# Attention scores from one wide moving operand, their halves summed on VectorE, and one layer's probabilities normalised on ScalarE

## The chip, the cores and the metric

The kernel runs on one core of one Trainium2 chip. The metric is the device time of the whole program in microseconds (us); lower is better. A number that names a line, such as L211, is a line of the kernel file.

## What is computed

A decoder trunk of two layers over 256 tokens of width 2048, in float32. Layer 0 is "forgetting attention" with 32 heads of 64; layer 1 is sliding-window attention with 32 query heads that share 4 key/value heads. Cut to what matters:

```python
for i in range(2):
    h = rmsnorm(x, norm_g[i])
    p = h @ w_in[i]                       # q, k, v and a gate (and, in layer 0, a forget column per head)
    # layer 0: s = q k^T / 8 + c[t] - c[s], causal; softmax; times v
    # layer 1: s = rope(q) rope(k)^T / 8, window of 128, a learned sink in the softmax; times v
    y = attention(q, k, v) * silu(gate)
    x = x + y @ w_out[i]
return rmsnorm(x, final_g)
```

## The kernel before

**Matrix products.** Every float32 operand is split into a high part, rounded to the matmul's own format (fp32r), and a low part, the remainder. A product is three terms: high by high, high by low, low by high. A weight piece arrives by DMA; ScalarE rounds it (`load`, L210, a CAST), VectorE subtracts to get the low part (L211), and the two lie side by side in a tile `w`. In `block` (L216) one stationary operand multiplies high and low of the other side at once, 512 columns wide, and then the stationary low part multiplies the high part, 256 columns wide: for a weight part of four 128-row slices this is 4 matmuls of 512 columns and 4 of 256. Both go into one bank of PSUM, whose second half, the high-by-low term, is copied out by ScalarE (`low_half`, L257) and added by VectorE.

**The order of the work.** The weights are one stream of units of 256 output columns. A unit has four parts and two halves of output columns (c = 0 and 1, 128 each). The main loop at the end of the kernel calls `block(u, p, 0)` for a new part and then `block` of the part before it for half 1. After every second matmul `tick` advances a clock of steps and runs what has been put down for that step with `after`. So a block is four steps. A head pair's attention work is put down this way in `Pair.later`: scores at step s, the transposes of the first head's probabilities at step t, those of the second at t + 4, and for the whole group of two pairs the product with the values at a third step. The steps count from the moment that half 0 of the k unit (layer 0) or of the q unit (layer 1) is complete, and stand in the tables at the top: `FOX_DUE = ((16, 34), (40, 60), 106)` means pair 0 at s = 16, t = 34, pair 1 at s = 40, t = 60, values at 106. `FOX_FIRST` and `FOX_LAST` serve layer 0's first and last group, `SWA_LAST` layer 1's last. A group of layer 0 has four units (q, k, gate, v), 128 steps; a group of layer 1 has two (q, gate), 64 steps. TensorE's matmuls keep the order of the program; on VectorE and ScalarE a scheduler sets the order when the program is built, and both then run strictly in that order.

**From q to scores in layer 1.** When a half of the q unit is done, `rotate` (L691 to L697) adds the two halves of PSUM, shuffles, multiplies by the two rope tables and adds, and `stack_q` stacks the high and low parts of the 64 rows of each head over each other in 128 partitions: two copies on ScalarE (L329), two subtractions on VectorE (L330). Half c of the q unit holds the two heads of pair c. In layer 0 the keys are treated alike after `k` (L456 to L464).

**Scores to probabilities.** `score` multiplies, for each of the two query blocks and each of the two heads, q's stacked operand by the keys' high part and then, into the same place, by their low part. The first query block sees 128 keys and the second 256: four matmuls of 128 columns and four of 256 for a pair of heads. `biased` (L299) then reads the sum from PSUM, adds bias or mask, scales, writes the tile `st` to SBUF and keeps the row maximum: four instructions of VectorE. The exponentials are four ScalarE instructions (L309), the normalisation a reciprocal and four multiplications by a column on VectorE (L317, L320). TensorE transposes `st` (L76, into `pt`), ScalarE copies the result out (L363), and `values` multiplies it by v (into `psy`).

**Buffers.** The scores have two banks of PSUM (`ps_s`), the transposes two, the accumulators four.

Of the kernel before, what the change touches and what calls it, by code (L numbers as in the profile page):

```python
# [46 lines left out]
LOWEST = -3.4e38  # L47
SCALE = HD ** -0.5
# [3 lines left out]
def trunk(  # L52
# [16 lines left out]
    nc = tc.nc  # L69


    def mm(*args, **kw):
        tc.keep_in_program_order(nc.tensor.matmul(*args, **kw))  # L73
# [31 lines left out]
    def after(steps, fn):  # L105
        due.setdefault(clock[0] + max(steps, 1), []).append(fn)
# [82 lines left out]
    state = {}  # L189
# [26 lines left out]
    def block(unit, p, c):  # L216
# [14 lines left out]

        first, last = kt0 == 0, kt0 + s == KT
        ops = [operands(i) for i in range(s)]
        if unit.halves:

# [54 lines left out]

    BLK = ((slice(0, P), 0), (slice(P, 3 * P), 1))

    def biased(pss, bias, scale):

        st = work.tile([P, 2, 3 * P], F32, tag="st", name="st")
        mx = work.tile([P, 2, 2], F32, tag="mx", name="mx")
        for hh in range(2):
            for rng, qb in BLK:
                nc.vector.tensor_tensor_reduce(  # L299
                    out=st[:, hh, rng], in0=pss[hh][:, rng], in1=bias(hh, rng), scale=scale,  # L300
                    scalar=LOWEST, op0=ALU.add, op1=ALU.max, accum_out=mx[:, qb, hh : hh + 1],
                )
        return st, mx
# [11 lines left out]
    def normalise(st, l):  # L315
        rl = work.tile([P, 2, 2], F32, tag="rl", name="rl")
        nc.vector.reciprocal(rl, l)  # L317
        for hh in range(2):
            for rng, qb in BLK:
                nc.vector.tensor_scalar_mul(st[:, hh, rng], st[:, hh, rng], rl[:, qb, hh : hh + 1])  # L320

# [8 lines left out]
            nc.vector.tensor_sub(q2[other, hh, :], t[w, :], q2[w, hh, :].bitcast(F32))  # L330
        return q2

    def score(pss, q2, kk):

        for rng, qb in BLK:
            keys = rng.stop - rng.start
            for hh in range(2):
                q = q2[:, hh, qb * P : (qb + 1) * P]
                for part in range(2):
                    mm(  # L340
                        pss[hh][:, rng], q, kk[hh][:, part, 0:keys],
                        start=part == 0, stop=part == 1,
                    )

    class Pair:


        def __init__(self, j, scores, prepare=None):
            self.j, self.scores, self.prepare = j, scores, prepare

        def early(self):
            self.bias = self.prepare()

        def s(self):
            self.st = self.scores()

        def t(self, hh, group):
            pt = ps_t.tile([P, 512], F32, tag="T", name="pt")
# [4 lines left out]
            nc.scalar.copy(group.pts[hh][:, self.j, :], pt[:, 0 : 3 * P])  # L363

        def later(self, group, s, t):
            if self.prepare is not None:
                after(s - BIAS, self.early)
# [38 lines left out]
    ones_row, z, a = (once[0:H, i * S : (i + 1) * S] for i in range(3))  # L406
# [33 lines left out]
    class FoxGroup(Group):  # L440
# [13 lines left out]
        def k(self, c, ps):  # L454
# [32 lines left out]
        def pair(self, j):  # L487
            h0 = 4 * self.g + 2 * j

            def bias():  # L490

                assert "forgot" in state
                bc = fox.tile([P, 2, 3 * P], F32, tag="bc", name="bc")
                nc.gpsimd.dma_start(out=bc, in_=negc_d[h0 : h0 + 2, :].partition_broadcast(P))  # L494
                for hh in range(2):
                    diagonal = bc[:, hh, :].rearrange("p (b k) -> p b k", k=P)[:, 0:3:2, :]
                    fill_where_not(diagonal, [[0, 2], [-1, P]], 0, 1)
                return bc

            def scores():  # L500
                pss = [ps_s.tile([P, 512], F32, tag="S", name="ps_s") for _ in range(2)]
                kk = self.kT[j]
                score(pss, self.qT[j], (kk[:, 0], kk[:, 1]))
                bc = made.bias
                st, mx = biased(pss, lambda hh, rng: bc[:, hh, rng], 1.0)
# [4 lines left out]
                normalise(st, exps(st, mx))  # L510
                return st

            made = Pair(j, scores, bias)
            return made

        def v_of(self, j, b, hh):
            return self.vg[b][:, (2 * j + hh) * HD : (2 * j + hh + 1) * HD]
# [198 lines left out]
    class SwaGroup(Group):  # L716
# [6 lines left out]
        def q(self, c, ps):  # L723
# [3 lines left out]
            if c == 0:  # L727
                self.attend(2 * self.u, SWA_LAST if self.u == 7 else SWA_DUE, self.u == 7, True)

        def pair(self, j):  # L730
            h0 = 4 * self.u + 2 * j
            kv = self.u // 2

            def scores():
                pss = [ps_s.tile([P, 512], F32, tag="S", name="ps_s2") for _ in range(2)]
                kk = state["kk"][:, kv]
                score(pss, self.qT[j], (kk, kk))
                st, mx = biased(pss, lambda hh, rng: smask[:, rng], SCALE)
# [8 lines left out]
                normalise(st, l)  # L747
                return st

            return Pair(j, scores)  # L750

        def v_of(self, j, b, hh):
            kv = self.u // 2
# [53 lines left out]
    start = [(u, p) for p in range(3) for u in (v0, q0, k0)]  # L807
# [25 lines left out]
    smask = cpool.tile([P, 3 * P], F32, name="smask")  # L833
# [86 lines left out]
```

## Time and profile before

| | |
|---|---|
| median of 3 runs | 844.64 us (844.48 to 844.76) |
| the profiled execution, its own time | 844.48 us |
| its span, from first to last instruction | 842.7 us |
| TensorE (PE) busy | 830.0 us, 98% |
| VectorE (DVE) busy | 656.7 us, 78% |
| ScalarE (ACT) busy | 542.6 us, 64% |
| GpSimd (POOL) busy | 67.8 us, 8% |
| mean granted TensorE clock | 0.997 |
| moved by DMA | 150.51 MB, 179 GB/s on average |

In the rows of the timeline the first number is the start in us from the start of the span and the second the time that the row covers; "x8" means that eight like instructions of one engine were merged, and the row then bears the first one's form. The records of matmuls overlap (their ends are modelled), so the pace of TensorE is read from one start to the next. In the rows of groups the numbers behind the bar are busy us, mean ns of one instruction, and idle us of the engine before them with what ended it.

### The profile page before, as it was taken

How to read it: one execution, taken by the hardware profiler on the slowest of the kernel's cores; microseconds unless marked ns; L12 is line 12 of the kernel's file. 1: busy time of each engine (PE TensorE's matmuls, PEld its weight loads, DVE VectorE, ACT ScalarE, POOL GpSimd, SP SyncE). 2: the span in 40 equal slices, each digit the busy share in tenths (PEclk: the TensorE clock that was granted, in tenths of full speed). 3: DMA queues.
4: the chain of work that ended last, by engine and by line, in shares of the span. 5: the costliest groups of instructions: out<-in, count | busy, mean ns of one | idle time of the engine just before them, and what ended most of it. 6: DMA issues, size and time to landing. Idle time of an engine off the chain costs nothing.

```text
span 842.7 us, 13456 instructions
## 1 busy us (share of the span) xinstructions
PE 830.0 (98%) x4972; PEld 720.9 (86%) x4972; DVE 656.7 (78%) x1380; ACT 542.6 (64%) x1061; POOL 67.8 (8%) x93
## 2 busy tenths in 40 slices
PE   8999999999999999999999999999999999999995
PEld 7888888888888888888888888888888888888885
DVE  6898868678686877867677778788898889877555
ACT  7678757667575765746555555567766776666562
POOL 1022001101010010100011110000000000003210
PEclk9999999999999999999999999999999999999998
DMA  8765555555465555554465554544444535364523
GB/s 300 258 218 214 188 187 171 186 192 189 159 227 161 171 209 166 196 177 154 160 211 192 198 195 158 188 159 139 161 150 151 164 137 174 126 203 163 191 100 101
DMA packets 27969, 150.51 MB, mean 179 GB/s; under 512 B 3152, under 2 KB 8176, under 8 KB 12288
## 3 DMA queue, kind: packets, MB, share of 16 engines
q1 hardware_dynamic: 24176, 141.94, 48.9%
q0 software_dynamic: 1408, 6.36, 2.4%
q10 hardware_dynamic: 2320, 1.35, 0.5%
q8 instruction: 39, 0.64, 0.3%
q14 instruction: 26, 0.21, 0.1%
HBM read 147.50 MB, written 2.15 MB: 178 GB/s over the span
## 4 chain that ended last, share of the span: by engine, by line
PE 94%; DVE 4%; ACT 1%; issue 1%; DMA 0%; ACTq 0%; DVEq 0%
PE acc L73 85%; PE ps_s L73 3%; PE psy L73 3%; PE pt L76 2%; DVE w L211 1%; ACT w L210 1%; DMA wraw<-in_vf_dram 0%; DVE st L299 0%; DVE xs L159 0%; DVE xT L667 0%; DVE ssq L784 0%; ACT st L309 0%; DVE q L330 0%; PE ps_n L73 0%; DVE st L320 0%
## 5 line engine op out<-in xcount | busy, mean ns | idle before, releaser
L73 PE MATMUL acc<-xs,w 128*128 128x512 f32 (+1 forms) x2624 | 483.2, 339 | 0.2 <-DVE w L211 0.2
L73 PEld LDWEIGHTS acc<-xs,w 128*128 128x128 f32 x2624 | 405.2, 189 | 59.9 <-issue 3.9
L211 DVE TENSOR_TENSOR w<-wraw,w 128x1024 fp32r<-128x1024 f32 (+3 forms) x271 | 325.1, 1204 | 108.1 <-ACT w L210 106.1
L210 ACT CAST w<-wraw 128x1024 fp32r<-128x1024 f32 (+3 forms) x271 | 277.3, 1028 | 133.3 <-PE acc L73 124.2
L73 PE MATMUL acc<-ys,w 128*128 128x512 f32 x960 | 170.8, 338 | 0.0
L73 PEld LDWEIGHTS acc<-ys,w 128*128 128x128 f32 x960 | 147.4, 189 | 21.5 <-issue 0.6
L73 PE MATMUL acc<-w,xs 128*128 128x256 f32 (+2 forms) x608 | 114.3, 335 | 2.5 <-DVE w L211 1.3
L73 PEld LDWEIGHTS acc<-w,xs 128*128 128x128 f32 x608 | 93.8, 189 | 14.6 <-DVE w L211 2.0
L257 ACT COPY half<-acc 128x256 f32<-128x256 f32 x112 | 41.2, 368 | 60.2 <-PE acc L73 59.3
L309 ACT ACTIVATE st<-st,mx 128x128 f32<-128x128 f32 (+1 forms) x128 | 56.6, 444 | 13.3 <-DVE mx L509 7.9
L576 POOL TENSOR_TENSOR acc<-acc,sq 128x256 f32<-128x256 f32 x28 | 29.9, 1069 | 105.2 <-ACT sq L570 105.2
L363 ACT COPY pts<-pt 128x384 f32<-128x384 f32 x64 | 30.4, 475 | 11.1 <-PE pt L76 11.1
L73 PE MATMUL ps_s<-kk,q 128*128 128x128 f32 (+1 forms) x256 | 35.7, 281 | 0.2
L320 DVE TENSOR_SCALAR st<-st,rl 128x128 f32<-128x128 f32 (+1 forms) x128 | 32.9, 320 | 1.1
L73 PEld LDWEIGHTS ps_s<-kk,q 128*128 128x128 f32 x256 | 32.1, 190 | 1.3 <-issue 0.4
L76 PE MATMUL pt<-ident,st 128*128 128x128 f32 x192 | 31.5, 273 | 0.0
L574 POOL COPY acc<-sq 128x256 f32<-128x256 f32 x2 | 1.9, 936 | 334.0 <-ACT sq L570 334.0
L125 POOL TENSOR_SCALAR_AFFINE_SELECT bc<-bc 128x256 f32<-128x256 f32 x32 | 22.9, 737 | 56.7 <-DMA bc<-negc_d 56.7
L494 POOL DMA_DIRECT2D bc<-negc_d x16 | 8.9, 555 | 214.9 <-DVE mx L508 176.7
L76 PEld LDWEIGHTS pt<-ident,st 128*128 128x128 f32 x192 | 23.2, 140 | 2.3
L159 DVE SCALAR_TENSOR_TENSOR xs<-xT,g_sb,xs 128x256 fp32r<-128x256 f32 x32 | 22.0, 712 | 3.8 <-ACT xs L158 3.8
L329 ACT CAST q<-qT 64x256 fp32r<-64x256 f32 x32 | 12.8, 401 | 18.6 <-DVE qT L697 18.2
(132 smaller groups left out, 578.4 us busy)
## 6 DMA issues: line engine op xcount, KB each, us to landing
wraw<-in_fox_in_dram SPq DMA_DIRECT2D x58, 1024.0 KB, 4.9
wraw<-in_swa_in_dram SPq DMA_DIRECT2D x36, 1024.0 KB, 4.9
wraw<-in_fox_out_dram SPq DMA_DIRECT2D x14, 1024.0 KB, 4.9
wraw<-in_swa_out_dram SPq DMA_DIRECT2D x14, 1024.0 KB, 4.9
bc<-negc_d POOLq DMA_DIRECT2D x16, 384.0 KB, 4.3
wraw<-in_fox_in_dram SPq DMA_DIRECT2D x6, 512.0 KB, 4.5
wraw<-in_fox_out_dram SPq DMA_DIRECT2D x4, 512.0 KB, 3.7
wraw<-in_swa_out_dram SPq DMA_DIRECT2D x4, 512.0 KB, 3.7
```

Of the source, the lines that this page charges most:

```text
L73: tc.keep_in_program_order(nc.tensor.matmul(*args, **kw))
L76: tc.keep_in_program_order(nc.tensor.transpose(out, in_, ident))
L125: nc.gpsimd.affine_select(out=ap, in_=ap, compare_op=ALU.is_ge, fill=NEG, base=base, pattern=pattern, channel_multiplier=mult,)
L159: nc.vector.scalar_tensor_tensor(out=xs[:, kt, 1, :], in0=xT[:, kt, :], scalar=g, in1=xs[:, kt, 0, :].bitcast(F32), op0=ALU.mult, op1=ALU. ...
L210: nc.scalar.copy(w[:, :, 0, :], raw)
L211: nc.vector.tensor_tensor(out=w[:, :, 1, :], in0=raw, in1=w[:, :, 0, :].bitcast(F32), op=ALU.subtract)
L257: nc.scalar.copy(s, ps[:, S : 2 * S])
L309: nc.scalar.activation(st[:, hh, rng], st[:, hh, rng], AF.Exp, bias=nm[:, qb, hh : hh + 1], accum_out=l[:, qb, hh : hh + 1],)
L320: nc.vector.tensor_scalar_mul(st[:, hh, rng], st[:, hh, rng], rl[:, qb, hh : hh + 1])
L329: nc.scalar.copy(q2[w, hh, :], t[w, :])
L363: nc.scalar.copy(group.pts[hh][:, self.j, :], pt[:, 0 : 3 * P])
L576: nc.gpsimd.tensor_add(sums[0], sums[0], s)
```

## The change

A score is now one matmul per head and query block: the keys' high and low parts, which lie next to each other, are one moving operand of 2 x 256 or 2 x 128 columns, and land side by side in PSUM. VectorE first adds the low half to the bias or mask into `st` and then runs the maximum instruction with the high half and `st`. The second query block comes first, at step s, with a bank for each head; the first block, both heads in one bank, follows `SECOND` = 8 steps later (`s_first`), and everything after the maxima hangs on this second call. In layer 1 alone, the four multiplications of `normalise` are ScalarE's. The tables of steps are new. Cut to its core:

```diff
-FOX_DUE = ((16, 34), (40, 60), 106)
-FOX_FIRST = ((46, 68), (74, 94), 114)
-FOX_LAST = ((14, 32), (38, 72), 86)
-SWA_DUE = ((16, 40), (44, 64), 74)
-SWA_LAST = ((26, 45), (30, 56), 68)
+FOX_DUE = ((14, 42), (46, 72), 106)
+FOX_FIRST = ((46, 74), (78, 100), 118)
+FOX_LAST = ((12, 38), (42, 72), 86)
+SWA_DUE = ((12, 40), (44, 72), 86)
+SWA_LAST = ((22, 50), (36, 64), 76)
+SECOND = 8
...
-                nc.vector.tensor_scalar_mul(st[:, hh, rng], st[:, hh, rng], rl[:, qb, hh : hh + 1])
+                p, r = st[:, hh, rng], rl[:, qb, hh : hh + 1]
+                if scalar:
+                    nc.scalar.mul(p, p, r)
+                else:
+                    nc.vector.tensor_scalar_mul(p, p, r)
...
-                for part in range(2):
-                    mm(
-                        pss[hh][:, rng], q, kk[hh][:, part, 0:keys],
-                        start=part == 0, stop=part == 1,
-                    )
...
+        def product(self, out, hh, qb, keys):
+            q2, kk = self.operands()
+            mm(out, q2[:, hh, qb * P : (qb + 1) * P], kk[hh][:, :, 0:keys], start=True, stop=True)
+        def reduce(self, high, hh, rng, qb):
+            st = self.st[:, hh, rng]
+            nc.vector.tensor_tensor_reduce(
+                out=st, in0=high, in1=st, scale=self.scale, scalar=LOWEST,
+                op0=ALU.add, op1=ALU.max, accum_out=self.mx[:, qb, hh : hh + 1],
+            )
         def s(self):
...
+            pss = [ps_s.tile([P, 512], F32, tag="S", name="ps_s") for _ in range(2)]
+            for hh in range(2):
+                self.product(pss[hh], hh, qb, S)
+            for hh in range(2):
+                nc.vector.tensor_add(self.st[:, hh, rng], pss[hh][:, S:], self.bias[:, hh, rng])
+                self.reduce(pss[hh][:, 0:S], hh, rng, qb)
+            after(SECOND, self.s_first)
+        def s_first(self):
...
+            for hh in range(2):
+                self.product(ps[:, hh], hh, qb, P)
+            nc.vector.tensor_add(self.st[:, :, rng], ps[:, :, 1, :], self.bias[:, :, rng])
+            for hh in range(2):
+                self.reduce(ps[:, hh, 0, :], hh, rng, qb)
+            self.soft(self.st, self.mx)
```

What the new tables do to the order is seen best in a middle group of layer 1. On TensorE, around the first scores of the group (`ps_s`, `ps_s2`), before: `acc_5996` is the second half of the q unit, `acc_6073` the gate unit, `pt` the transposes of the previous group, `psy` its values.

```order
L76 MATMUL pt_6065<-ident_244,st_5949 128x128 x3
L73 MATMUL acc_6073<-xs_80,w_5985 128x512 x4
L73 MATMUL acc_6073<-xs_80,w_5985 128x256 x4
L73 MATMUL acc_5996<-xs_80,w_5907 128x512 x4
L73 MATMUL psy_6086<-pts_5923,vs_5356 64x512
...
L73 MATMUL acc_5996<-xs_80,w_5907 128x256 x4
L73 MATMUL acc_6073<-xs_80,w_6005 128x512 x4
L73 MATMUL acc_6073<-xs_80,w_6005 128x256 x4
L73 MATMUL ps_s2_6126<-kk_5236,q2_6052 128x128 x2
L73 MATMUL ps_s2_6127<-kk_5236,q2_6052 128x128 x2
```

And now, with `acc_5973` for the second half of the q unit and `acc_6063` for the gate unit:

```order
L78 MATMUL pt_6072<-ident_244,st_5939 128x128 x3
L75 MATMUL acc_5973<-xs_80,w_5907 128x512 x4
L75 MATMUL acc_5973<-xs_80,w_5907 128x256 x4
L78 MATMUL pt_6085<-ident_244,st_5939 128x128 x3
L75 MATMUL ps_s_6092<-kk_5236,q2_6047 128x512
L75 MATMUL ps_s_6093<-kk_5236,q2_6047 128x512
L75 MATMUL acc_6063<-xs_80,w_6005 128x512 x4
L75 MATMUL acc_6063<-xs_80,w_6005 128x256 x4
```

The scores have moved ahead by a whole block and the values product, the previous group's transposes have moved back by two blocks, and only three transposes stand between the last matmul of the q unit and the scores.

On VectorE, at the same place, the steps that make the first pair's operand, before: `rot_t_6043`, `rot_6047`, `qT_6042` and `q2_6052` belong to pair 0, and `rot_t_6099` and `rot_6103` to pair 1.

```order
L211 TENSOR_TENSOR w_6026<-wraw_6024,w_6026 128x4x256
L691 TENSOR_TENSOR rot_t_6043<-acc_5910,half_6044 128x256
L693 STREAM_SHUFFLE rot_6047<-rot_t_6043 128x256
L694 TENSOR_TENSOR rot_t_6043<-rot_t_6043,rope_c_5208 128x256
L695 TENSOR_TENSOR rot_6047<-rot_6047,rope_c_5208 128x256
L211 TENSOR_TENSOR w_6070<-wraw_6024,w_6070 128x4x256
L697 TENSOR_TENSOR qT_6042<-rot_t_6043,rot_6047 128x256
L330 TENSOR_TENSOR q2_6052<-qT_6042,q2_6052 64x256 x2
...
L691 TENSOR_TENSOR rot_t_6099<-acc_5996,half_6100 128x256
L693 STREAM_SHUFFLE rot_6103<-rot_t_6099 128x256
```

And now, with `rot_t_6038`, `rot_6042`, `qT_6037` and `q2_6047` for pair 0 and `rot_t_6101` and `rot_6105` for pair 1:

```order
L213 TENSOR_TENSOR w_6026<-wraw_6024,w_6026 128x4x256
L706 TENSOR_TENSOR rot_t_6038<-acc_5910,half_6039 128x256
L213 TENSOR_TENSOR w_6060<-wraw_6024,w_6060 128x4x256
L708 STREAM_SHUFFLE rot_6042<-rot_t_6038 128x256
L706 TENSOR_TENSOR rot_t_6101<-acc_5973,half_6102 128x256
L709 TENSOR_TENSOR rot_t_6038<-rot_t_6038,rope_c_5208 128x256
L710 TENSOR_TENSOR rot_6042<-rot_6042,rope_c_5208 128x256
L708 STREAM_SHUFFLE rot_6105<-rot_t_6101 128x256
L712 TENSOR_TENSOR qT_6037<-rot_t_6038,rot_6042 128x256
L709 TENSOR_TENSOR rot_t_6101<-rot_t_6101,rope_c_5208 128x256
L710 TENSOR_TENSOR rot_6105<-rot_6105,rope_c_5208 128x256
L324 TENSOR_TENSOR q2_6047<-qT_6037,q2_6047 64x256 x2
```

Pair 1's first four steps have moved in among pair 0's, and the first of them reads `acc_5973`, the accumulator that TensorE completes just ahead of the transposes and scores above. The six middle groups of layer 1 all have these rows.

More of the change, by code (lines that the diff above doesn't have):

```diff
@@ L291, in trunk @@
     BLK = ((slice(0, P), 0), (slice(P, 3 * P), 1))
[L293 to L301, printed above, removed]
-                )
-        return st, mx
     def exps(st, nm):
@@ L313, in exps, with normalise @@
         return l
-    def normalise(st, l):
+    def normalise(st, l, scalar):
         rl = work.tile([P, 2, 2], F32, tag="rl", name="rl")
@@ L331, in stack_q, with __init__ @@
         return q2
[L333 to L338, printed above, removed]
-                for part in range(2):
-                    mm(
-                        pss[hh][:, rng], q, kk[hh][:, part, 0:keys],
-                        start=part == 0, stop=part == 1,
-                    )
     class Pair:
-        def __init__(self, j, scores, prepare=None):
-            self.j, self.scores, self.prepare = j, scores, prepare
+        def __init__(self, j, operands, scale, soft, prepare):
+            self.j, self.operands, self.scale, self.soft = j, operands, scale, soft
+            self.prepare = prepare
@@ new lines, in s @@
+        def s(self):
+            self.st = work.tile([P, 2, 3 * P], F32, tag="st", name="st")
+            self.mx = work.tile([P, 2, 2], F32, tag="mx", name="mx")
+            rng, qb = BLK[1]
+            pss = [ps_s.tile([P, 512], F32, tag="S", name="ps_s") for _ in range(2)]
[5 more added lines that the diff above has]
+            after(SECOND, self.s_first)
@@ L357, in t @@
+        def s_first(self):
+            rng, qb = BLK[0]
+            ps = ps_s.tile([P, 512], F32, tag="S", name="ps_s")
+            ps = ps.rearrange("p (h a k) -> p h a k", h=2, k=P)
+            for hh in range(2):
[4 more added lines that the diff above has]
+            self.soft(self.st, self.mx)
         def t(self, hh, group):
@@ L365, in later @@
         def later(self, group, s, t):
-            if self.prepare is not None:
-                after(s - BIAS, self.early)
+            after(s - BIAS, self.early)
             after(s, self.s)
@@ L498, in bias, with soft @@
                 return bc
[L500 to L505, printed above, removed]
+            def soft(st, mx):
                 c2 = cq[:, :, h0 : h0 + 2]
@@ L509, in scores, with operands @@
                 nc.vector.tensor_sub(mx, c2, mx)
[L510 to L514, printed above, removed]
+                normalise(st, exps(st, mx), False)
+            def operands():
+                kk = self.kT[j]
+                return self.qT[j], (kk[:, 0], kk[:, 1])
+            return Pair(j, operands, 1.0, soft, bias)
         def v_of(self, j, b, hh):
@@ L732, in pair, with soft @@
             kv = self.u // 2
[L734 to L738, printed above, removed]
+            def soft(st, mx):
                 sk = sink[:, h0 : h0 + 2].unsqueeze(1).to_broadcast([P, 2, 2])
@@ L746, in scores, with operands @@
                 nc.vector.tensor_add(l, l, es)
-                normalise(st, l)
-                return st
-            return Pair(j, scores)
+                normalise(st, l, True)
+            def operands():
+                kk = state["kk"][:, kv]
+                return self.qT[j], (kk, kk)
+            mask = smask.unsqueeze(1).to_broadcast([P, 2, 3 * P])
+            return Pair(j, operands, SCALE, soft, lambda: mask)
         def v_of(self, j, b, hh):
```

1 line of the change is left out of this document (removed).

## The prediction

> **What bounds the kernel now.** I read the page first, then what TensorE waits for, then the timeline of a middle group of each layer.
>
> ```profile
> span 842.7 us, 13456 instructions
> ...
> PE 830.0 (98%) x4972; PEld 720.9 (86%) x4972; DVE 656.7 (78%) x1380; ACT 542.6 (64%) x1061; POOL 67.8 (8%) x93
> ...
> PEclk9999999999999999999999999999999999999998
> ...
> PE 94%; DVE 4%; ACT 1%; issue 1%; DMA 0%; ACTq 0%; DVEq 0%
> ```
>
> The row for its stream of weights in TensorE's waits (total us, count, longest):
>
> ```profile
> PE acc L73 <- DVE w L211: 1.4, 3, 0.9
> ```
>
> TensorE is busy for 98% of the span, 94% of the chain that ended last is its own work, and its longest total wait in the stream of weights is 1.4 us. So the end is set by TensorE's stream: what shortens it is gained in full, as long as VectorE and ScalarE still deliver ahead of it, and every wait that is put into it is lost in full. Both have idle time on average; whether it lies in the right place is the question.
>
> **TensorE's own work.** A pair's scores, and blocks for the price of wider matmuls, in a group of layer 0:
>
> ```profile
> 137.45 1.09 PE L73 MATMUL ps_s<-kk,q 128*128 128x128 f32 x8
> 138.37 6.70 PE L73 MATMUL acc<-xs,w 128*128 128x512 f32 x36
> ...
> 145.71 1.10 PE L73 MATMUL acc<-w,xs 128*128 128x512 f32 x4
> 146.65 0.49 PE L76 MATMUL pt<-ident,st 128*128 128x128 f32 x3
> ...
> 149.76 5.78 PE L73 MATMUL acc<-w,xs 128*128 128x512 f32 x32
> 155.37 0.49 PE L76 MATMUL pt<-ident,st 128*128 128x128 f32 x3
> ```
>
> Start to start, eight score matmuls take 138.37 - 137.45 = 0.92 us, 115 ns each, though half of them have 128 columns and half 256. Four of 512 columns take 146.65 - 145.71 = 0.94, 235 ns each. Four blocks of four 512s and four 256s take 155.37 - 149.76 = 5.61, so 1.40 a block and (1.40 - 0.94) / 4 = 115 ns for one of 256 columns. The new scores are two of 512 and two of 256: 2 x 235 + 2 x 115 = 700 ns. A pair saves 0.22 us, the 32 pairs (256 score matmuls before) 7.1 us.
>
> [...]
>
> **What moves on the other engines.** The nearest rows:
>
> ```profile
> L281 DVE TENSOR_TENSOR gt<-acc,half 128x256 f32<-128x256 f32 x32 | 13.4, 420 | 1.7 <-ACT half L257 1.6
> L320 DVE TENSOR_SCALAR st<-st,rl 128x128 f32<-128x128 f32 (+1 forms) x128 | 32.9, 320 | 1.1
> L618 ACT ACTIVATE xT<-xT,g_sb 128x256 f32<-128x256 f32 x14 | 7.2, 511 | 0.4
> L652 ACT ACTIVATE diag<-ident,tail 128x128 f32<-128x128 f32 x2 | 0.8, 403 | 0.2
> ```
>
> VectorE gets three additions of 256 columns out of PSUM per pair, 3 x 0.42 x 32 = 40 us, and loses half of L320's 32.9, 16 us: +24 on 656.7, 81% of the span. ScalarE gets 32 multiplications of 256 columns and 32 of 128: 32 x (0.511 + 0.403) = 29 us on 542.6. Spread evenly both are hidden by TensorE's stream, and I cost them at nothing except where a due step is close. There they count.
>
> **The first scores of a layer 1 group.** This is the group before, TensorE, VectorE, ScalarE:
>
> ```profile
> 639.32 0.49 PE L76 MATMUL pt<-ident,st 128*128 128x128 f32 x3
> 639.57 1.64 PE L73 MATMUL acc<-xs,w 128*128 128x512 f32 x8
> 641.04 0.49 PE L76 MATMUL pt<-ident,st 128*128 128x128 f32 x3
> 641.29 2.57 PE L73 MATMUL acc<-xs,w 128*128 128x512 f32 x12
> ...
> 647.20 1.09 PE L73 MATMUL ps_s<-kk,q 128*128 128x128 f32 x8
> ```
>
> ```profile
> 639.44 2.35 DVE L211 TENSOR_TENSOR w<-wraw,w 128x1024 fp32r<-128x1024 f32 x2
> 641.72 0.42 DVE L691 TENSOR_TENSOR rot_t<-acc,half 128x256 f32<-128x256 f32 x1
> ...
> 642.18 0.45 DVE L693 STREAM_SHUFFLE rot<-rot_t 128x256 f32<-128x256 f32 x1
> 642.66 0.43 DVE L694 TENSOR_TENSOR rot_t<-rot_t,rope_c 128x256 f32<-128x256 f32 x1
> 643.00 0.42 DVE L695 TENSOR_TENSOR rot<-rot,rope_c 128x256 f32<-128x256 f32 x1
> 643.34 1.22 DVE L211 TENSOR_TENSOR w<-wraw,w 128x1024 fp32r<-128x1024 f32 x1
> 644.48 0.42 DVE L697 TENSOR_TENSOR qT<-rot_t,rot 128x256 f32<-128x256 f32 x1
> 645.37 0.87 DVE L330 TENSOR_TENSOR q<-qT,q 64x256 fp32r<-64x256 f32 x2 [0.47 <-ACT q L329]
> ```
>
> ```profile
> 637.98 1.98 ACT L210 CAST w<-wraw 128x1024 fp32r<-128x1024 f32 x2
> 639.87 0.36 ACT L257 COPY half<-acc 128x256 f32<-128x256 f32 x1
> 640.13 0.47 ACT L363 COPY pts<-pt 128x384 f32<-128x384 f32 x1
> 641.24 1.05 ACT L210 CAST w<-wraw 128x1024 fp32r<-128x1024 f32 x1 [0.64 <-PE acc L73]
> ...
> 644.93 0.83 ACT L329 CAST q<-qT 64x256 fp32r<-64x256 f32 x2 [2.26 <-DVE qT L697]
> ```
>
> The operand is complete at 645.37 + 0.87 = 646.24, 0.96 us ahead of the scores at 647.20. In the new order the scores stand one block (1.40 us) and the values product earlier, right behind the transposes that the previous group's probabilities feed. ScalarE now has, in this order, those four multiplications, a weight cast, the copy `half` of q's first half, the copy of the transposed probabilities, a second weight cast, and only then the `half` of q's second half. VectorE has pair 1's addition, which waits for that last copy, ahead of pair 0's rope multiplications.
>
> The walk, from the start of the first transposes as 0, with start-to-start times from the rows (a cast 0.95 to 1.05, a weight subtraction 1.14, an independent VectorE step of 256 columns 0.34): the multiplications end at about -0.3. This comes from pair 1's low-block scores, 20 steps or 5 x 1.40 = 7.0 us ahead: 0.3 latency, 0.9 addition and maxima, 0.2, 1.2 weight subtraction, 0.2, 1.9 exponentials, 0.5 gate and reciprocal, 1.5 multiplications make 6.7. ScalarE: cast to 0.65, copy to 0.95, copy to 1.3, cast to 2.25, second `half` to 2.6. VectorE: the second tile's subtraction 2.3 to 3.45, shuffle to 3.8, pair 1's addition to 4.15, two rope multiplications to 4.8, pair 1's shuffle to 5.15, the sum `qT` to 5.6. ScalarE's two casts end at 6.05 and 6.45, VectorE's two subtractions at 6.5 and 6.9. TensorE, from the rows above, would reach the scores at 0.25 + 1.47 + 0.25 = 1.97 and the second one at 2.2; it starts that at 6.95. **A wait of 4.75 us, in six groups alike, 28.5 us.**
>
> From below: with no backlog at all, the path from q's last matmul (1.72) through `half` (2.4), five VectorE steps, cast, cast and subtraction ends at 5.6, still 3.45 us of waiting. From above 5.5, with 0.1 us more at each of the hand-overs. I take the walk's value, since its queue order is given.
>
> **The other due steps.** Layer 1's first and layer 0's middle groups:
>
> ```profile
> 537.51 0.87 DVE L330 TENSOR_TENSOR q<-qT,q 64x256 fp32r<-64x256 f32 x2 [0.47 <-ACT q L329]
> 538.40 1.08 PE L73 MATMUL ps_s<-kk,q 128*128 128x128 f32 x8
> ...
> 236.40 0.42 DVE L464 TENSOR_TENSOR kk<-k,kk 64x256 fp32r<-64x256 f32 x1
> 236.82 1.09 PE L73 MATMUL ps_s<-kk,q 128*128 128x128 f32 x8
> ```
>
> Layer 1's first group has no probabilities ahead of it, and its order is unchanged: the second score would come at 538.40 - 1.40 + 0.23 = 537.23 and its operand at 538.38, a wait of 1.2 us. In its last group the scores (step 22) lie behind three blocks, half of another and the values product, which nearly covers the 6.95 us; but VectorE's gate product, which waits for the values, stands between the two operands: 1.7 us, bounds 0 and 3. In layer 0 the second head's keys are done at 236.82, just ahead of their use 0.29 us into the scores; two steps (four 256s, 0.46) earlier that is 0.28 us late in six groups, 1.7, and in the last group, two steps of 512s (0.94), about 0.9. The probabilities have 20 steps instead of 18 for pair 0 and 18 instead of 20 for pair 1, near enough to nothing; bounds 0 and 3 us in all. The two score banks are freed by VectorE within 2 us against eight steps, 2.8 us: nothing.
>
> **The sum.** -7.1 + 28.5 + 1.2 + 1.7 + 2.6 = +26.9 us. The profiled execution took 844.48 us, its span 842.7, and the median of the runs is 844.64: **871.4 us**.
>
> **Rivals.** *Only the bare path counts* (ScalarE and VectorE reach q's second half without backlog): 6 x 3.45 = 20.7, small terms halved to 2.8: 861. Against it: the casts and copies are in the queue.
>
> *TensorE's clock falls in the waits.* The granted clock (PEclk, tenths) is 9 in every slice but the last, where TensorE's work runs out, so no wait of this length is in the trace. If a wait of 4.75 us brought half clock for as long again, each would cost 2.4 more, 14 in six: 886. [...]
>
> *The waits don't arise* and the shorter stream stands alone, -7.1 plus the small terms of layer 0 at most: 838 to 840. This is decided at the scores of layer 1: the operand must be there 2.2 us after the transposes began. For it speaks the slack of 0.96 us before; against it that the path starts at 1.72 with a matmul of TensorE itself. Nothing I know closes that gap, except an order read wrongly.
>
> **Chances.** Forecast (862 to 880) 0.62; bare path and below (847 to 862) 0.14; clock (880 to 892) 0.15; shorter stream 0.07; something within the bound 0.02. A measurement of this kernel tells about 0.2%, 1.7 us. The range, 854 to 887, leaves out the shorter stream, the ends of the bare path and of the clock. Faster 0.07, same 0.02, slower 0.91.
>
> **What would show it.** In the changed profile TensorE's waits should have a new first row, scores on VectorE's q2 subtraction, seven or eight times, the longest near 4.8 us, about 30 in total; each ps_s group's start-to-start time should be 0.70 over its four matmuls where it does not wait; VectorE should idle ahead of pair 1's addition until ScalarE's `half`. I am wrong if these waits stay under 2 us, if the four matmuls take 0.9, or if the time goes into layer 0.

## The result and the profile after

| | before | changed |
|---|---|---|
| median of six runs | 844.75 us (844.48 to 845.0) | 890.58 us (888.42 to 891.31) |
| ratio, with its 95% interval | | 1.0538 (1.0524 to 1.0552) |
| profiled execution, own time | 844.48 us | 888.84 us |
| mean granted TensorE clock | 0.997 | 0.976 |

The kernel became slower by 45.8 us. The sign and the place were as forecast, the size was not: 871.4 was predicted, with a range up to 887.

The page of the changed kernel, with the same four rows as before:

```profile
span 886.8 us, 13301 instructions
...
PE 842.0 (95%) x4844; PEld 721.3 (81%) x4844; DVE 672.0 (76%) x1412; ACT 563.5 (64%) x1125; POOL 63.3 (7%) x93
...
PEclk9999999999999999999999999998898898999998
...
PE 79%; DVE 10%; ACT 7%; issue 2%; DMA 1%; ACTq 0%; DVEq 0%; SPq 0%
```

TensorE issues 128 matmuls fewer and is yet busy 12 us longer (842.0 against 830.0), and its share of the chain has fallen from 94% to 79%. The row of the clock says why a smaller stream takes longer: from the 28th slice on there are 8s among the 9s. TensorE's waits (total us, count, longest) have the new first row that was forecast:

```profile
PE ps_s L75 <- DVE q L324: 28.6, 9, 4.4
...
PE ps_s L75 <- DVE kk L482: 1.8, 7, 0.4
...
PE pt L78 <- DVE st L314: 1.4, 1, 1.4
```

One middle group of layer 1 on TensorE, from one product with the values (`psy`) to the next:

```profile
610.92 1.52 PE L75 MATMUL psy<-pts,vs 128*64 128x512 f32 x8
...
631.12 0.49 PE L78 MATMUL pt<-ident,st 128*128 128x128 f32 x3
...
632.85 0.49 PE L78 MATMUL pt<-ident,st 128*128 128x128 f32 x3
637.75 1.22 PE L75 MATMUL ps_s<-kk,q 128*128 128x512 f32 x2 [4.41 <-DVE q L324]
638.77 4.87 PE L75 MATMUL acc<-xs,w 128*128 128x512 f32 x16
643.47 0.40 PE L75 MATMUL ps_s<-kk,q 128*128 128x256 f32 x2
...
644.73 1.52 PE L75 MATMUL psy<-pts,vs 128*64 128x512 f32 x8
```

The same two rows in the kernel before:

```profile
562.19 1.52 PE L73 MATMUL psy<-pts,vs 128*64 128x512 f32 x8
589.39 1.52 PE L73 MATMUL psy<-pts,vs 128*64 128x512 f32 x8
```

A group took 27.20 us and now takes 644.73 - 610.92 = 33.81: 6.61 more, though it waits only 4.41 and should have saved 0.44. So some 2.6 us of a group are neither waiting nor more work. The stretches of the group before it show them (after the bounds: length, PE busy, PEld, DVE, ACT and POOL, then the granted clock, the DMA share and GB/s):

```profile
598.58:601.99 3.41, 1.21 (x9) 0.90 (x7) 3.37 (x8) 2.69 (x5) 0.00 (x0) 1.00 0.02 7
601.99:605.41 3.42, 1.19 (x3) 0.96 (x4) 3.33 (x10) 1.20 (x3) 0.00 (x0) 0.50 0.85 299
605.41:608.82 3.41, 3.41 (x12) 2.83 (x11) 2.89 (x9) 0.41 (x2) 0.00 (x0) 0.50 0.00 0
608.82:612.24 3.42, 3.42 (x21) 2.06 (x19) 2.10 (x7) 1.05 (x1) 0.00 (x0) 1.00 0.00 0
```

There the wait ran from 599.8 to 604.2. From 601.99 to 608.82 the granted clock is 0.50, and TensorE worked 1.19 + 3.41 = 4.60 us of that at the slower pace. Inside such stretches a matmul of 512 columns starts 0.427 us after the one before it and one of 256 columns 0.213; outside them the trace has 0.233 and 0.119 at the median. (In the rows above, two blocks take 643.47 - 638.77 = 4.70 us, mostly inside a stretch, where they take 2 x 1.40 otherwise.) So about 45% of the time worked there is lost, here 2.1 us of the 2.6. The clock's records show such stretches after each of the six waits: they begin at 571.27, 602.00, 636.13, 670.26, 704.39 and 738.53 us, 9 or 10 times 3.413 us apart, and last 3.41 us the first time and 6.83 after that. TensorE worked 3.41, 4.60, 5.21, 5.51, 5.66 and 5.75 us in them, 30.1 in all, of which 45%, 13.6 us, is lost.

Layer 0 is read from one pair of matmuls that both kernels have at the start of layer 1's norm, first before, then changed:

```profile
505.77 0.59 PE L73 MATMUL ps_n<-acc,ones 128*128 128x256 f32 x2
```

```profile
508.02 0.59 PE L75 MATMUL ps_n<-acc,ones 128*128 128x256 f32 x2
```

It comes 2.25 us later, where the shorter stream of its 16 pairs alone would bring it 3.5 earlier (16 x 0.22): 5.8 us went to waits and small stalls in layer 0, against 2.6 forecast. The rows of waits hold 3.7 of them: 1.4 for `st`, 1.8 for the second head's keys and 0.5 for a `half`. The keys in one of the changed kernel's middle groups:

```profile
188.40 0.40 PE L75 MATMUL ps_s<-kk,q 128*128 128x512 f32 x1
189.02 0.47 PE L75 MATMUL ps_s<-kk,q 128*128 128x512 f32 x1 [0.23 <-DVE kk L482]
```

### The profile page after: what moved, and what is told of

The parts are those of the page before. It is cut to its first block, busy times and chain, and to the rows that moved or that the text cites. A ratio compares the mean times of both kernels' runs of the same rounds, so it can differ in the third digit from the quotient of the medians.

```text
span 886.8 us, 13301 instructions
## 1 busy us (share of the span) xinstructions
PE 842.0 (95%) x4844; PEld 721.3 (81%) x4844; DVE 672.0 (76%) x1412; ACT 563.5 (64%) x1125; POOL 63.3 (7%) x93
## 4 chain that ended last, share of the span: by engine, by line
PE 79%; DVE 10%; ACT 7%; issue 2%; DMA 1%; ACTq 0%; DVEq 0%; SPq 0%
PE acc L75 71%; DVE w L213 4%; PE ps_s L75 3%; PE psy L75 2%; ACT st L299 2%; PE pt L78 2%; ACT w L212 2%; ACT st L312 1%; DMA xT<-in_xt_dram 1%; DVE q L324 1%; DVE rot L708 1%; DVE rot_t L709 1%; DVE st L346 1%; DVE rot L710 1%; DMA wraw<-in_fox_in_dram 0%
## 5 line engine op out<-in xcount | busy, mean ns | idle before, releaser
L75 PE MATMUL acc<-xs,w 128*128 128x512 f32 (+1 forms) x2624 | 496.5, 344 | 0.2 <-DVE w L213 0.2
L75 PEld LDWEIGHTS acc<-xs,w 128*128 128x128 f32 x2624 | 416.1, 193 | 62.9 <-issue 3.3
L75 PE MATMUL acc<-w,xs 128*128 128x256 f32 (+2 forms) x608 | 112.3, 333 | 1.9 <-DVE w L213 1.3
L75 PE MATMUL ps_s<-kk,q 128*128 128x256 f32 (+1 forms) x128 | 40.2, 386 | 30.9 <-DVE q L324 28.6
L75 PEld LDWEIGHTS ps_s<-kk,q 128*128 128x128 f32 x128 | 22.8, 197 | 39.1 <-issue 32.9
L346 DVE CUSTOM_DVE_ANT_0 st<-ps_s,st 128x128 f32<-128x128 f32 (+1 forms) x128 | 40.4, 352 | 0.6
L299 ACT ACTIVATION_READ_ACCUMULATOR st<-st,mx 128x1 f32 x128 | 24.1, 188 | 0.0
```

Of the source, the lines that this page charges most:

```text
L299: nc.scalar.activation(st[:, hh, rng], st[:, hh, rng], AF.Exp, bias=nm[:, qb, hh : hh + 1], accum_out=l[:, qb, hh : hh + 1],)
L346: nc.vector.tensor_tensor_reduce(out=st, in0=high, in1=st, scale=self.scale, scalar=LOWEST, op0=ALU.add, op1=ALU.max, accum_out=self.mx[:, ...
```

## The experiments

**Is the slow stretch the clock, and is it the idling that brings it?** The first kernel fills the wait with needless work.

```diff
+            if self.j == 0:
+                _, kk = self.operands()
+                for _ in range(self.fill):
+                    mm(pss[0], kk[0][:, 0, 0:P], kk[0], start=True, stop=True)
             for hh in range(2):
                 self.product(pss[hh], hh, qb, S)
...
+            made.fill = 18 if 0 < self.u < 7 else 0
```

> The changed kernel with 18 needless matmuls of 512 columns (18 x 235 ns = 4.2 us) ahead of the first scores of each of the six middle groups of layer 1: they use the keys alone and write the bank that the scores then overwrite, so TensorE works where it stood idle and the scores start no earlier. Theory: the clock falls because TensorE idles, so the half-clock stretches (15 us of TensorE's work in six) go and nothing else: 875.5 us (873 to 878), clock 0.99 or above. Rival, the slow stretch belongs to the wide scores or to what VectorE and the DMAs do at that time: it stays, 888 to 893, clock near 0.975.

Measured: 876.45 us (876.09 to 876.87), 14.1 less than the changed kernel, clock 0.997 against 0.976. Its TensorE at the same place:

```profile
598.35 4.36 PE L75 MATMUL ps_s<-kk 128*128 128x512 f32 x18
602.94 1.01 PE L75 MATMUL ps_s<-kk,q 128*128 128x512 f32 x2 [0.23 <-DVE q L324]
```

The scores start 602.94 - 598.11 = 4.8 us after the second transposes (598.11 in this trace), as in the changed kernel (637.75 - 632.85 = 4.9). The operand comes no earlier; only the idleness is gone, and 14.1 us go with it between the medians, 886.8 - 874.4 = 12.4 between the spans of the profiled executions, about the 13.6 worked out above. That the half clock comes from TensorE idling is shown.

**How much idling does it take?** The same fill with 0, 3, 6, 9, 12 and 15 matmuls in the six groups.

> As the fill with 18 needless matmuls, but with 0, 3, 6, 9, 12 and 15 of them in the six middle groups in order, so that TensorE stands idle 4.4, 3.7, 3.0, 2.3, 1.6 and 0.9 us. In the changed kernel the half clock began at times that lie whole multiples of 3.41 us apart and held for whole stretches of 3.41. Theory, the clock is set for each such stretch by how much of the one before TensorE idled, and 60% is enough: the half clock appears for certain at 4.4 and 3.7 us, by the place of the grid at 3.0 and 2.3, and never at 1.6 or 0.9; 880 to 887 us. Rival, only a stretch that is idle throughout brings it: at 4.4 us at most, nearly always nowhere else: 876 to 879.

Measured: 886.79 us in its only run, mean clock 0.983. The half clock followed the gaps of 4.41, 3.62 and 2.93 us (6.83 us of it each time), not the one of 2.25, yet the one of 1.57 (3.41 us of it), and not 0.85: 23.9 us together, where the mean clock gives 885.0 x 2 x 0.017 = 30 us at half with the run's end in it. The theory's "never at 1.6" fell. The two stretches of 3.41 us in which the 2.25 and the 1.57 lay, and the one behind each:

```profile
671.08:674.49 3.41, 1.97 (x9) 1.29 (x7) 3.41 (x11) 1.71 (x4) 0.00 (x0) 1.00 0.38 94
674.49:677.91 3.42, 2.56 (x12) 2.03 (x13) 3.30 (x11) 1.28 (x4) 0.00 (x0) 1.00 0.51 213
...
705.22:708.63 3.41, 1.80 (x7) 1.19 (x7) 3.32 (x10) 1.58 (x4) 0.00 (x0) 1.00 0.71 279
708.63:712.04 3.41, 3.41 (x14) 2.92 (x13) 2.58 (x7) 0.04 (x1) 0.00 (x0) 0.50 0.00 0
```

Of the gap of 2.25 us, 1.44 lie in the first of these stretches, which was idle for 42%, and the clock stayed at 1.00 behind it; the 1.57 lie wholly in the third, idle for 47%, and behind it the clock was 0.50. So the length of the wait alone did not decide it. Nor does the idle share of the stretch ahead set these cases apart: in the run of the normalisation alone (below) the stretch from 566.24 to 569.65, idle for 55% (TensorE worked 1.52 of 3.41 us), had a clock of 1.00 behind it, and the one from 596.96 to 600.37, idle for 63% (1.26 of 3.41), had 0.50. What decides between these four, no run shows. In the changed kernel the stretches just ahead of the six falls were idle for 96, 65, 82, 91, 96 and 99%. Its first stretch at half clock, in which TensorE worked throughout, had the full clock behind it; in the first stretch after each of the other five falls TensorE worked 1.19 to 2.34 of the 3.41 us, and a second one at half clock followed, in which it worked throughout, before the clock was full again. So five of the six waits cost two stretches.

**Does the wait come from the step at which the scores stand?** First from the other side: the kernel before, with only the table `SWA_DUE` changed, which serves all groups of layer 1 but the last.

```diff
-SWA_DUE = ((16, 40), (44, 64), 74)
+SWA_DUE = ((12, 40), (44, 72), 86)
```

> The kernel before with the changed table for layer 1's middle groups alone (scores at 12 and 44, transposes at 40 and 72, values at 86); the scores, their sums and the normalisation are the old ones. Theory: the early step is enough for a wait, the operand coming about 6.9 us after step 0 (as in the kernel before) and TensorE arriving 4.9 us after it: 2 us (1.5 to 3) in six or seven groups, 12 to 18 us, with clock loss between 0 and 9: 861 us (853 to 872). Rival, the waits need the wide operand or the normalisation on ScalarE: under 0.5 us each, 843 to 848.

Measured: 885.72 us, ratio 1.0487 (1.0471 to 1.0503). The steps alone cost 41 us, 24.6 more than the theory had; the whole change costs 45.8, with the gain of the shorter stream in it. The waits were 3.76 us, not the 2 of the theory, and the mean clock was 0.976, as in the changed kernel (VectorE's order is one microsecond of the wait, as the run with that order pinned shows, below):

```profile
600.95 1.46 PE L73 MATMUL ps_s<-kk,q 128*128 128x128 f32 x5 [3.76 <-DVE q L330]
```

Then the changed kernel, with the scores moved behind the operand.

```diff
-SWA_DUE = ((12, 40), (44, 72), 86)
-SWA_LAST = ((22, 50), (36, 64), 76)
+SWA_DUE = ((28, 56), (54, 82), 96)
+SWA_LAST = ((28, 50), (36, 62), 74)
```

> The changed kernel with layer 1's first scores put down 16 steps later (28 instead of 12, everything of a layer 1 group behind them moved along; layer 1's last group 28 instead of 22). Theory: the whole loss of layer 1 is TensorE standing at the first scores of a group for an operand that comes about 9.4 us after step 0, and the half clock that follows; at step 28 TensorE arrives after the operand, so the six waits of 4.4 us, the six stretches at half clock and the two small waits of the first and last group go: 843 us (841 to 846), mean granted clock 0.99 or above. Rival, VectorE and ScalarE cannot carry the additions and the normalisation at TensorE's pace, so that the wait only moves to the transposes or the values: 852 to 875, with a new row of TensorE's waits on st or pts.

Measured: 852.83 us, ratio 1.0098 (1.0083 to 1.0113), clock 0.997. No wait on q2 is left in the middle groups and no half clock: 37.8 of the 45.8 us are gone. But it is the rival's number, and TensorE's first wait row says a part of why, 3.8 of the 9.8 us above the theory:

```profile
PE pt L78 <- ACT st L312: 3.8, 8, 0.7
```

The transposes of the second pair now stand ahead of ScalarE's multiplications, in each of the eight groups. That row holds only the bare waits: a middle group takes 628.56 - 600.82 = 27.74 us in this trace, 0.97 more than in the tuned kernel below. So the tables were moved once more, in both layers, and twice, since the first set left two waits (1.5 us for the last values at the output weights, 1.1 us for the second group's keys).

```diff
-FOX_DUE = ((14, 42), (46, 72), 106)
-FOX_FIRST = ((46, 74), (78, 100), 118)
-FOX_LAST = ((12, 38), (42, 72), 86)
-SWA_DUE = ((12, 40), (44, 72), 86)
-SWA_LAST = ((22, 50), (36, 64), 76)
+FOX_DUE = ((16, 44), (46, 72), 106)
+FOX_FIRST = ((46, 76), (68, 98), 114)
+FOX_LAST = ((16, 42), (44, 72), 88)
+SWA_DUE = ((28, 58), (54, 88), 102)
+SWA_LAST = ((28, 54), (42, 68), 78)
```

The first set had `FOX_FIRST` ((46, 76), (78, 106), 120) and `SWA_LAST` ((28, 56), (44, 72), 84).

> The changed kernel with every table moved to what the runs so far showed: layer 1's first scores at step 28, its transposes 22 and 26 steps behind the low-block scores (58 and 88), values at 102, last group 28/56, 44/72, 84; in layer 0 first scores at 16 instead of 14, the first group's second pair transposed at 106 instead of 100, the last group's scores at 16. Theory: with the waits on q2, kk and st gone, the shorter stream stands alone, 32 pairs by 0.22 us: 844.6 - 7.1 = 837.5 us (835.5 to 840), TensorE's waits as few as in the kernel before. Rival, ScalarE's multiplications stay late for the transposes, or the additions hold up VectorE: 841 to 850.

Measured: 840.63 us, ratio 0.9949 (0.9937 to 0.9962), between theory and rival. Then the set shown:

> The tuned kernel with the two waits that were left in it moved away from: layer 1's last group takes its values at 78 instead of 84 (scores 28 and 42, transposes 54 and 68), so that the output weights do not wait 1.5 us for them, and layer 0's first group treats its second pair at 68, 98 instead of 78, 106, so that its transposes and their copies no longer stand ahead of the second group's keys (1.1 us). Theory: 840.6 - 2.6 = 838.0 us (836.5 to 839.5), the shorter stream nearly in full. Rival, the waits move to the next step in line in these two places: 840 to 841.

Measured: **837.83 us** (837.22 to 838.06), ratio 0.9917 (0.9904 to 0.9931), 0.8% faster than the kernel before: a small gain, but clear of its interval. Its TensorE in a group, from one product with the values to the next, with scores and what follows them; the last two rows are the wide scores of the other pair:

```profile
569.61 1.52 PE L75 MATMUL psy<-pts,vs 128*64 128x512 f32 x8
...
595.11 0.40 PE L75 MATMUL ps_s<-kk,q 128*128 128x256 f32 x2
595.35 1.09 PE L75 MATMUL acc<-xs,w 128*128 128x512 f32 x4
596.38 1.52 PE L75 MATMUL psy<-pts,vs 128*64 128x512 f32 x8
...
603.53 0.63 PE L75 MATMUL ps_s<-kk,q 128*128 128x512 f32 x2
604.00 1.56 PE L75 MATMUL acc<-xs,w 128*128 128x256 f32 x8
```

Two matmuls of 512 columns take 604.00 - 603.53 = 0.47 us and two of 256 take 0.24, together 0.71. A group takes 26.77, 0.43 less than before. The sum's first term, 7.1 us, is there to within 0.2 as soon as hardly anything waits.

**What makes the operand late?** The changed kernel with VectorE normalising:

```diff
-                normalise(st, l, True)
+                normalise(st, l, False)
```

> The changed kernel with layer 1's normalisation back on VectorE. Theory: ScalarE's four multiplications (1.5 us) stand ahead of the weight cast and of the copy of q's first half, which VectorE waits for, so they make 1.0 to 1.5 us of the 4.4 us wait; VectorE's own four multiplications fall into its idle time there. The wait shrinks to 2.9 to 3.5 us, the clock still falls in most groups: 879 us (873 to 885). First rival, the normalisation on ScalarE is the cause of the waits as such: they shrink under 1 us, 845 to 855. Second rival, it has nothing to do with it, since the path from q's second half binds: 888 to 892.

Measured: 878.91 us (876.28 to 879.32), ratio 1.0401 (1.0385 to 1.0416), and a wait of 3.29:

```profile
601.15 1.22 PE L75 MATMUL ps_s<-kk,q 128*128 128x512 f32 x2 [3.29 <-DVE q L324]
```

So having the four multiplications on ScalarE makes 1.1 us of the 4.4. How they come into the path is seen in the changed kernel on VectorE and on ScalarE, in the group whose scores start at 637.75:

```profile
631.67 1.23 DVE L213 TENSOR_TENSOR w<-wraw,w 128x1024 fp32r<-128x1024 f32 x1 [1.73 <-ACT w L212]
...
633.25 1.23 DVE L213 TENSOR_TENSOR w<-wraw,w 128x1024 fp32r<-128x1024 f32 x1
...
634.73 0.42 DVE L706 TENSOR_TENSOR rot_t<-acc,half 128x256 f32<-128x256 f32 x1
...
636.07 0.42 DVE L712 TENSOR_TENSOR qT<-rot_t,rot 128x256 f32<-128x256 f32 x1
...
637.19 0.87 DVE L324 TENSOR_TENSOR q<-qT,q 64x256 fp32r<-64x256 f32 x2
```

```profile
629.20 1.50 ACT L312 ACTIVATE st<-st,rl 128x128 f32<-128x128 f32 x4
630.60 1.03 ACT L212 CAST w<-wraw 128x1024 fp32r<-128x1024 f32 x1
631.54 0.36 ACT L259 COPY half<-acc 128x256 f32<-128x256 f32 x1
...
633.13 0.36 ACT L259 COPY half<-acc 128x256 f32<-128x256 f32 x1
```

VectorE idles 1.73 us for a weight cast that stands behind the multiplications; the first `half` is copied only at 631.54, and all that follows is shifted. At the second pair's addition (634.73), where the prediction looked for idle time, there is none: its `half` had been ready since 633.49.

The same edit to the kernel before, with its own tables:

> The kernel before with layer 1's normalisation on ScalarE and nothing else changed. Theory: the four multiplications take 1.5 us on ScalarE, end about 0.5 us later than VectorE's did and stand ahead of the casts and of the copy of q's first half, which have 0.4 us of room at the transposes and 0.96 us at the scores: 0.3 to 1.5 us in each of seven groups, 850 us (846 to 856). Rival, the scheduler puts the casts first and nothing is late: 844 to 845.5.

Measured: 873.96 us, ratio 1.0343 (1.0324 to 1.0362): 29 us where 5 were expected, with waits of up to 2.33 us and a mean clock of 0.984 instead of 0.997.

```profile
600.54 1.68 PE L73 MATMUL ps_s<-kk,q 128*128 128x128 f32 x6 [2.33 <-DVE q L334]
```

The operand had 0.96 us of room and came 3.3 us later, twice what four multiplications take. On VectorE, between pair 0's last rope steps and its two subtractions, this kernel has:

```profile
629.43 0.69 DVE L399 TENSOR_TENSOR gt<-psy,gt 128x512 f32<-128x512 f32 x1
...
630.49 0.42 DVE L695 TENSOR_TENSOR rot_t<-acc,half 128x256 f32<-128x256 f32 x1
...
631.44 1.23 DVE L211 TENSOR_TENSOR w<-wraw,w 128x1024 fp32r<-128x1024 f32 x1
632.58 0.68 DVE L401 TENSOR_TENSOR ys<-gt,ys 128x512 fp32r<-128x512 f32 x1
633.30 0.87 DVE L334 TENSOR_TENSOR q<-qT,q 64x256 fp32r<-64x256 f32 x2
```

The gate product, the other pair's addition, a weight subtraction and the values' subtraction stand there; in the kernel before the two subtractions came right behind the sum `qT`. But VectorE's order is not the whole of it, since its subtractions need ScalarE's two copies of `qT`:

```profile
631.30 0.62 ACT L400 CAST ys<-gt 128x512 fp32r<-128x512 f32 x1
631.82 0.83 ACT L333 CAST q<-qT 64x256 fp32r<-64x256 f32 x2
```

In the kernel before, the copies began 0.45 us after the start of the sum (644.93 - 644.48), ScalarE standing idle for it; here they begin 631.82 - 630.04 = 1.78 after it, behind a weight cast and the cast of `ys`. The first copy ends at about 632.2, and VectorE, busy with its long steps, takes its subtraction up 1.0 us later. So ScalarE's 1.5 us let short, urgent steps fall behind long ones on both engines. No run pins the order in this kernel, so how the 3.3 us divide is read from the trace alone.

Is the order on VectorE a cause by itself? In two kernels pair 1's addition was put behind pair 0's last subtraction, by an edge that orders and waits for nothing. First with the steps alone:

```diff
...
-        nc.vector.tensor_add(t, ps[:, 0:S], low_half(ps))
+        add = nc.vector.tensor_add(t, ps[:, 0:S], low_half(ps))
+        if behind is not None:
+            tc.add_manual_dep(
+                add.ins, behind.ins.name,
+                mybir.DependencyInfo(mybir.DependencyClass.NoSync, mybir.DependencyReason.DATA),
+                reason="order",
+            )
...
+            rotate(ps, [(t, slice(0, P))], state["sub"] if c == 1 else None)
```

> The kernel before with the changed steps for layer 1 (as in the run of the steps alone, 885.7 us, waits of 3.76), and VectorE's first step on the second half of q ordered behind the last subtraction that makes the first pair's operand. In the run of the steps alone four such steps of the second pair (0.34 us each) stand between the first pair's sum and its subtractions. Theory, VectorE's order is the rest of that wait: it shrinks by about 1.1 us, to 2.4 to 2.9, the weight subtraction staying in front; with the clock falling in fewer groups 872 us (864 to 880). Rival, ScalarE's casts bind and the order of VectorE changes nothing: 883 to 887, waits of 3.6 or more.

Measured: 875.09 us, ratio 1.0361 (1.0345 to 1.0376), the wait now 2.79 instead of 3.76:

```profile
599.04 2.10 PE L73 MATMUL ps_s<-kk,q 128*128 128x128 f32 x8 [2.79 <-DVE q L330]
```

One microsecond of that wait was VectorE's order. Then in the changed kernel:

> The changed kernel with the same order on VectorE. Here the scheduler moves a weight subtraction (1.14 us, its cast at hand) into the place that two steps of the second pair (0.67 us) leave. Theory, the wait stays or grows a little, 4.2 to 4.9 us: 890 us (887 to 893). Rival, the second pair's addition, which waits for the last copy out of the second half, is what holds the operand: the wait shrinks under 3.8 us, 882 to 886.

Measured: 896.21 us, ratio 1.061 (1.0592 to 1.0627), slower than the changed kernel:

```profile
605.89 1.22 PE L75 MATMUL ps_s<-kk,q 128*128 128x512 f32 x2 [4.80 <-DVE q L324]
```

The wait grew by 0.4 us as the theory said. The total went 3 us past it, because layer 1's last group got a wait of 3.06 us there; the mean clock was 0.971 where the changed kernel had 0.976. What VectorE does in the freed place, a weight subtraction of 1.14 us, is longer than the two steps of the second pair that stood there, so this run does not say what the operand would do with the place left empty. That the second pair's addition waited for nothing is seen above, at 634.73.

**Does it matter where the normalisation is, when no step is close?** The two tuned kernels with VectorE normalising:

> The same tables with layer 1's normalisation on VectorE. Theory, where no step is close the engine does not matter: within 1.5 us of the tuned kernel with ScalarE's, 837.5 us. Rival, the 30 us that ScalarE was given back are VectorE's limit in layer 1 (it has the additions now): 841 or more. Other rival, ScalarE's multiplications were the last thing late: at least 2 us less than the tuned kernel with them.

> The same with layer 1's normalisation on VectorE. Theory, the 2 us between the two tuned kernels lay at the values of the last group and in the half clock after it, which both kernels now avoid: within 0.8 us of the kernel with ScalarE's. Rival, VectorE's 30 us count along the way: 839.5 or more.

Measured: 842.63 us, ratio 0.9972 (0.9963 to 0.9982), and 839.16, ratio 0.9935 (0.9922 to 0.9947), against 840.63 and 837.83 with ScalarE. Both missed their theory. The first differs by 2.0 where 1.5 were allowed and lies in the range of its first rival; but its trace puts the difference in one place, the last values, for which TensorE waits 2.2 us instead of 1.5, and the mean clock was 0.994 instead of 0.998. The second differs by 1.3, more than the 0.8 expected, and all of it lies at the same place of the last group:

```profile
PE acc L75 <- DVE ys L415: 1.6, 1, 1.6
```

This wait of TensorE for the last values is not in the kernel with ScalarE; the same matmuls lie within about half a microsecond of each other up to it. So the engine does not matter along the way, and the 40 us of additions on VectorE cost nothing either.

## Why the prediction was wrong, point by point

**What bounds the kernel**: right. Every microsecond put into TensorE's stream was lost, and the 6.9 us of the tuned kernel are those taken out of it.

**TensorE's own work**: right, 0.71 us for a pair's four matmuls (0.47 and 0.24 in the tuned kernel's trace) where 0.70 was worked out.

**The work on the other engines, hidden except near a due step**: right. The tuned kernels show the cover, the others the due steps.

**The walk to the first scores**: right within 0.35 us. It had the scores 6.95 us after the first transposes and a wait of 4.75; they started 637.75 - 631.12 = 6.63 after them and waited 4.41. One reading in it was wrong, though it moved no number: VectorE was to idle ahead of pair 1's addition. It idled earlier, for the weight cast; the addition, at 634.73, found a `half` that had been ready since 633.49.

**The half clock**: this is the step that failed. It was left out of the sum and stood among the rivals, with a chance of 0.15. Its price there, 2.4 us a wait and 14 in six, was close to the 13.6 found, and its place was right. What was wrong was the ground on which it was put low: that no row of before showed a fall. In the changed kernel each of the six waits of 4.4 us had half clock behind it, the stretch of 3.41 us ahead of it being idle for 65 to 99%. That the trace of before shows no fall ahead of its last slice said nothing, since TensorE has no wait over 1.1 us there; and the last slice held a sign. Its stretches, in the same columns as above:

```profile
833.99:837.41 3.42, 0.46 (x2) 0.30 (x2) 2.29 (x9) 1.41 (x5) 0.00 (x0) 1.00 0.42 128
837.41:840.82 3.41, 0.00 (x0) 0.00 (x0) 1.54 (x5) 0.00 (x0) 0.00 (x0) 0.50 0.88 261
```

The one wait of 2.5 us lies in the first of them, which was idle for 87% and not throughout, and the half clock followed.

**Layer 0**: the keys were put 0.28 us late; the changed kernel's second head started 189.02 - 188.40 = 0.62 us after the first instead of 0.23, so at least 0.39 a group. And "20 steps instead of 18 for pair 0 and 18 instead of 20 for pair 1" is not true of the first group, whose table leaves the second pair 14 steps (86 to 100) where it had 20: there TensorE waited 1.4 us for `st`. That term was put at nothing.

**The sum**, over the profiled executions (+44.4):

| term | forecast | measured |
|---|---|---|
| shorter stream | -7.1 | -6.9 (the tuned kernel) |
| six waits of layer 1 | 28.5 | 26.5 (6 x 4.41) |
| half clock | 0 | 13.6 |
| layer 0 | 2.6 | 5.8 |
| layer 1's first and last group | 2.9 | 2.5 (waits of 0.82 and 0.35, 0.28 and 1.01) |
| together | 26.9 | 41.5 |

The remaining 2.9 us are not placed. The half clock and layer 0, together 16.8 us more than forecast, are nearly all of the 17.5 us by which the sum fell short.

**The rivals**: "only the bare path" fell, since the backlog of ScalarE was real. "The shorter stream alone", 838 to 840, was nothing the tables of the change could give; the tuned kernel's 837.83 is that case.

## What to carry to other kernels

Where one engine is busy 98% of the time, the place at which a step is put down is worth more than its work: here a table that asks for one layer's scores four steps earlier, and for its transposes and values later, cost 41 us, and a quarter of the scores' matmul time saved brought 7. When moving such a step, walk the operand's path through each engine's queue in the new order; when an engine gets new work, look not at its length but at what small, urgent steps will stand behind it. And a wait of TensorE is not priced by its length alone: here six waits of 4.4 us, 26.5 us in all, cost 13.6 more by the half clock that followed each of them.

## What the hardware showed that was not expected

In the changed kernel's trace the granted clock of TensorE was 1.00 or 0.50 and changed only at times that lie whole multiples of 3.413 us apart: it was 0.50 for 3.41 us behind the first of the six waits of 4.41 us and for 6.83 behind each of the other five. With these waits filled with needless matmuls the mean clock was 0.997 instead of 0.976. At 0.50 a matmul of 512 columns started 0.427 us after the one before it instead of 0.233, not quite twice as long. A wait of 4.41 us so cost up to 7.0 (with 45% of the 5.75 us that TensorE worked at half clock behind the last of them). And four multiplications on ScalarE, 1.5 us together, made the operand of the kernel before 3.3 us late, since the order on ScalarE and VectorE changed behind them.
